# A seven-product output projection in a one-core fp32 encoder step

## The chip, the cores and the metric

The kernel runs on one core of a Trainium2 chip. The metric is the device time of one execution in microseconds. The parts of the core that matter here are TensorE (PE in the profile, with its weight loads as PEld), VectorE (DVE), ScalarE (ACT), GpSimd (POOL) and the queue on SyncE that issues the DMAs (SPq).

## The reference

One layer of a streaming encoder for 1024 prompt frames and 32 sample frames (together 1056 columns), 1024 channels. Cut to what matters here:

```
ya = (o_attn * silu(ga)) @ w_pa
yb = (silu(layernorm(conv)) * silu(gb)) @ w_pb
m  = sigmoid(ma) * ya + sigmoid(mb) * yb
y  = x + m @ w_out
```

All of it is fp32. The input projections, the attention and the depthwise convolution come ahead of these lines and are not touched.

## The kernel before

Activations lie with the channels on the 128 partitions, in eight tiles (`KT = 8`) of 1056 frames (`TT`). An fp32 operand is held as a high part and a low part, both fp32r: ScalarE writes the high part (a cast), and GpSimd or VectorE writes the remainder (a subtraction). A product of two fp32 operands is then three matmuls: high by high, low weight by high, high weight by low. One output tile of 128 channels takes 8 contraction tiles x 3 chunks of 352 frames (`CH`) x 3 matmuls = 72 matmuls, each with its own 128x128 weight load.

The end of the kernel is three such projections, each run by `outproj(g, rh, rl, mk)` over eight output tiles: `pa` (the attention branch), `pb` (the convolution branch) and `out`. In the first tile of each the contraction loop is outside the chunk loop; the other seven go through `proj`, chunk by chunk. `load_raw` (L85) brings a 512 KB weight tile by DMA into one of three rotating buffers; `split_w` casts it to `wh` on ScalarE (L91) and writes `wl` on GpSimd in three pieces (L94). The closure that `mk` returns empties PSUM:

- `mk_pa` (L1170) scales a chunk and stores it to DRAM (`s_ya`).
- `mk_pb` loads a gate tile `smb` and a `ya` tile into the pool `bg` (five buffers of 1056 frames, handed out by `big`). For each chunk VectorE does a multiply out of PSUM (L1187) and an addition (L1188) into `smb`, ScalarE writes the high part `mh` (L1189), GpSimd the low part `ml` (L1190). `mh` and `ml` are the mixed input m (doubled) of the output projection.
- `mk_out` loads the residual `xres`, adds half of the PSUM chunk to it on VectorE (L1200), and stores the chunk to `yT` (L1201).

`pb` reads its input `c_h`, `c_l` from the pool `xp`, in which the normalised input lay earlier. PSUM has eight banks, seven in `pj3` and one in `pq`; each chunk takes one.

TensorE's instructions run in the order in which they are written (`manual_schedule`). Behind the attention, the order on the other engines and on the DMA queue is set by a scheduler by priority: inside `tc.high_priority(offset=n)` an instruction counts as written n instructions earlier (2000 for weights, 4000 for emptying PSUM). A tile waits only for the readers and writers of the memory that it takes over (`reuse_waits="tile"`).

Of the kernel before, what the change touches and what calls it, by code (L numbers as in the profile page):

```python
# [8 lines left out]
F32 = mybir.dt.float32  # L9
F32R = mybir.dt.float32r  # L10
BF16 = mybir.dt.bfloat16
AF = mybir.ActivationFunctionType
ALU = mybir.AluOpType
# [5 lines left out]
TT = T + TS  # L19
# [3 lines left out]
KT = 8  # L23
CH = 352
# [5 lines left out]
LNEXP = "natural_log_exp_and_others"  # L30
NFILL = 22
R_U, R_V, R_QK, R_G, R_A = 0.25, 0.17, 0.19, 0.27, 0.12
NWARM = 46
SAT = (2, 6, 10, 14)
SKEYS = PAST + TS
# [9 lines left out]
WSP = ((0, 3), (3, 6), (6, 8))  # L45
# [3 lines left out]
def build(tc, xT, xt, wv, wf, ckT, cv, clT, stT, vec, cst, yT, kT, vO, lfO, cpT, csT):  # L49
    nc = tc.nc  # L50
# [3 lines left out]
    def pool(name, bufs=1, stack=es, **kw):  # L54
        return stack.enter_context(tc.tile_pool(name=name, bufs=bufs, reuse_waits="tile", **kw))
# [16 lines left out]
    wp = pool("wp", 2)  # L72
    lnp = pool("lnp")
    mean = lnp.tile([128, TT], F32, name="mean")
    rstd = lnp.tile([128, TT], F32, name="rstd")
    rawp = [wp]

    def f32(ap):
        return ap.bitcast(F32)

    def load_raw(key, offset=2000):
        with tc.high_priority(offset=offset):
            rawp.append(rawp.pop(0))
            raw = rawp[-1].tile([128, KT, 128], F32, name="raw", tag="raw", bufs=1)
            nc.sync.dma_start(raw, wf[WIDX[key]])  # L85
        return raw

    def split_w(raw, offset=2000):
        with tc.high_priority(offset=offset):
            wh = wp.tile([128, KT, 128], F32R, name="wh", tag="wh")  # L90
            nc.scalar.copy(wh, raw)  # L91
            wl = wp.tile([128, KT, 128], F32R, name="wl", tag="wl")
            for k0, k1 in WSP:
                nc.gpsimd.tensor_sub(wl[:, k0:k1, :], raw[:, k0:k1, :], f32(wh[:, k0:k1, :]))  # L94
        return wh, wl

    def mms(ps, w, rh, rl, sl, kts=range(KT), first=True, last=True):
        wh, wl = w
        n, N = 0, 3 * len(kts)
        for kt in kts:  # L100
            for a, b in ((wh, rh), (wl, rh), (wh, rl)):
                nc.tensor.matmul(ps, a[:, kt, :], b(kt, sl), start=(first and n == 0), stop=(last and n == N - 1))  # L102
                n += 1

    def csl(c):
        return slice(c * CH, (c + 1) * CH)
# [53 lines left out]
    def proj(*a):  # L160
        for _ in steps(*a):
            pass


    xp = pool("xp")
    xh = xp.tile([128, KT, TT], F32R, name="xh", tag="h")
    xl = xp.tile([128, KT, TT], F32R, name="xl", tag="l")
    X = lambda kt, sl: xh[:, kt, sl]
    XL = lambda kt, sl: xl[:, kt, sl]
    sg = pool("sg")  # L170

    def t352(name, bufs):
        return sg.tile([128, CH], F32, name=name, tag=name, bufs=bufs)
# [5 lines left out]
    class Banks:  # L179

        n = 0
# [5 lines left out]
    pj = Banks()  # L187
# [145 lines left out]
    order = ExitStack()  # L333
# [3 lines left out]
    with tc.high_priority(offset=9000):  # L337
# [11 lines left out]
        warm = tr.tile([128, 512], F32, name="warm", tag="tr")  # L349
        for i in range(NWARM):  # L350
            nc.tensor.matmul(warm[:, :256], idle[:, :128], idle[:, :256], start=(i == 0), stop=(i == NWARM - 1))

# [25 lines left out]
    half = slice(0, D // 2), slice(D // 2, D)  # L378
# [111 lines left out]
    V, G = nc.vector, nc.gpsimd  # L490
# [32 lines left out]
    z = zp.tile([128, 9, H], F32, name="z")  # L523
# [45 lines left out]
    for c in range(4):  # L569
# [15 lines left out]
        for t in range(8):  # L585
            ps = pj.tile([128, 512], F32, name="pjv", tag="pj")
            n = 0
            for kt in range(KT):
                sl = slice(t * 128, t * 128 + 128)
                wh, wl = wh2[kt // 4][:, kt % 4, :], wl2[kt // 4][:, kt % 4, :]  # L590
# [174 lines left out]
    def gate_steps(g, f, pj):  # L765
        def ev(c, sl, ps):
            t = t352("t", 3)
            if g == "ga":
                sides["silu"] = nc.scalar.activation(t, ps, AF.Silu)
            else:  # L770
                nc.scalar.copy(t, ps)  # L771
            nc.sync.dma_start(s_g[g][f, :, sl], t)

        return steps((g, f), X, XL, pj, ev)

    class Head:
        def __init__(self, h):
            self.h = h
# [306 lines left out]
    p3 = ExitStack()  # L1085
# [5 lines left out]
    class Banks3:  # L1091
        n = 0
# [3 lines left out]
            return (pq if self.n % 8 == 0 else pj3).tile(*a, **k)  # L1096

    pjC = Banks3()
    sg2 = pool("sg2", 4, stack=p3, side="right")
    bg = pool("bg", 5, stack=p3, side="right")  # L1100
    rawp.extend(pool(f"rw{i}", 1, stack=p3, side="right") for i in range(2))

    def big(name):
        return bg.tile([128, TT], F32, name=name, tag="big")
# [29 lines left out]
    def last_gate():  # L1134
        for _ in gate_steps(*fills.pop(0), pj3):
            pass
# [2 lines left out]
        a_half(f)  # L1139
    while fills:  # L1140
        last_gate()

    def ln_step(f):
        for g in LNO[f - 1]:
            ln_out(g)

    def outproj(g, rh, rl, mk, between=lambda f: None):

        w = split_w(load_raw((g, 0)))
        pss = [pjC.tile([128, CH], F32, name="pj", tag="pj") for _ in range(3)]  # L1150
        for kt in range(KT):
            for c in range(3):
                mms(pss[c], w, rh, rl, csl(c), range(kt, kt + 1), kt == 0, kt == KT - 1)
        ev = mk(0)
        with tc.high_priority(offset=4000):
            for c in range(3):
                ev(c, csl(c), pss[c])
        for f in range(1, 8):
            between(f)
            proj((g, f), rh, rl, pjC, mk(f))  # L1160


    def mk_pa(f):
# [8 lines left out]
        return ev  # L1172

    outproj("pa", lambda kt, sl: ah[:, kt, sl], lambda kt, sl: al[:, kt, sl], mk_pa, ln_step)
    ch_, cl_ = chl
    mh = pap.tile([128, KT, TT], F32R, name="mh", tag="h")
    ml = pap.tile([128, KT, TT], F32R, name="ml", tag="l")

    def mk_pb(f):
        smb = big("smb")  # L1180
        nc.sync.dma_start(smb, s_g["mb"][f])
        nc.scalar.activation(smb, smb, AF.Tanh, scale=0.5)
        ya = big("ya")
        nc.sync.dma_start(ya, s_ya[f])

        def ev(c, sl, ps):
            nc.vector.scalar_tensor_tensor(smb[:, sl], smb[:, sl], 1.0, ps, op0=ALU.add, op1=ALU.mult)  # L1187
            nc.vector.tensor_add(smb[:, sl], smb[:, sl], ya[:, sl])  # L1188
            nc.scalar.copy(mh[:, f, sl], smb[:, sl])  # L1189
            nc.gpsimd.tensor_sub(ml[:, f, sl], smb[:, sl], f32(mh[:, f, sl]))  # L1190
        return ev

    outproj("pb", lambda kt, sl: ch_[:, kt, sl], lambda kt, sl: cl_[:, kt, sl], mk_pb)

    def mk_out(f):
        xres = big("xres")
        nc.sync.dma_start(xres, xT[:, f, :])

        def ev(c, sl, ps):
            nc.vector.scalar_tensor_tensor(xres[:, sl], ps, 0.5, xres[:, sl], op0=ALU.mult, op1=ALU.add)  # L1200
            nc.sync.dma_start(yT[f, :, sl], xres[:, sl])  # L1201
        return ev

    outproj("out", lambda kt, sl: mh[:, kt, sl], lambda kt, sl: ml[:, kt, sl], mk_out)
    p3.close()
    es.close()

# [81 lines left out]
```

## Time and profile before

| what | us |
|---|---|
| median of 3 runs (1393.85 to 1394.35) | 1393.89 |
| span of the profiled execution, first to last instruction | 1392.1 |
| median less span: what lies around the span | 1.8 |
| PE busy in the span | 1384.3 |
| `pa`, first to last matmul that reads `ah` | 1109.7 to 1202.7 |
| `pb`, first to last matmul that reads `c_h` | 1203.1 to 1294.6 |
| `out`, first to last matmul that reads `mh` | 1295.0 to 1388.0 |

The profiled execution has no device time of its own beside its span, so its span is set against the median of the runs. A matmul's duration in the trace includes its way through the array, and consecutive matmuls overlap; what one costs in a row of them is the distance between starts.

### The profile page before, as it was taken

To read this page: it belongs to the slowest core of one execution; us is meant where nothing else is said; L and a number is where in the kernel's file an instruction comes from. 1 tells how busy PE (TensorE), PEld (TensorE's weight loads), DVE (VectorE), ACT (ScalarE), POOL (GpSimd) and SP (SyncE) were. 2 spreads that over 40 slices of the span, in tenths; PEclk is the share of its full clock that TensorE was granted. 3 is DMA by queue.
4 is the path that set the end of the run, shared out by engine and by line. 5 is a ranking of instruction groups with operands and counts; after the bars stand their busy time and mean duration, and the time that the engine had idled before them with its cause. 6 is when DMAs were issued, how large, how long until landed. Compare 5 with 4: busy or idle time off the path is not lost.

```text
span 1392.1 us, 24733 instructions
## 1 busy us (share of the span) xinstructions
PE 1384.3 (99%) x9382; PEld 1346.1 (97%) x9382; DVE 906.5 (65%) x1280; ACT 642.7 (46%) x1318; POOL 623.2 (45%) x669
## 2 busy tenths in 40 slices
PE   8999999999999999999999999999999999999999
PEld 7999999999999999999999999999999999999998
DVE  6687787888898999657766767655555487132111
ACT  6333434646464642245555556655555556222100
POOL 2324254657575875443333444343433257254320
PEclk9999999999999999999999999999999999999999
DMA  5253442424342374344545556454642779444431
GB/s 182 93 179 116 153 136 97 155 85 144 98 164 88 124 207 141 116 124 123 144 137 169 155 147 175 118 152 124 174 134 86 266 265 289 135 150 141 143 107 47
DMA packets 110615, 201.24 MB, mean 145 GB/s; under 512 B 17377, under 2 KB 74593, under 8 KB 110497
## 3 DMA queue, kind: packets, MB, share of 16 engines
q1 hardware_dynamic: 110352, 199.60, 45.7%
q8 instruction: 74, 1.21, 0.4%
q14 instruction: 45, 0.36, 0.1%
q10 hardware_dynamic: 144, 0.07, 0.0%
HBM read 129.78 MB, written 69.84 MB: 143 GB/s over the span
## 4 chain that ended last, share of the span: by engine, by line
PE 97%; DVE 1%; ACT 1%; DMA 0%; issue 0%; POOL 0%; SPq 0%; DVEq 0%; POOLq 0%; ACTq 0%
PE pj L102 71%; PE pjv L592 7%; PE ptr L966 5%; PE po L982 3%; PE po L983 3%; PE psS L938 3%; PE psS L939 2%; PE psS L941 1%; PE pst L716 1%; PE pst L715 1%; PE ptx L434 0%; DMA xtok<-xt 0%; ACT xh L436 0%; PE pjs L549 0%; DVE xl L437 0%
## 5 line engine op out<-in xcount | busy, mean ns | idle before, releaser
L102 PE MATMUL pj<-xh,wh 128*128 128x352 f32 (+2 forms) x1536 | 509.3, 332 | 0.4 <-ACT t L771 0.3
L102 PE MATMUL pj<-xl,wh 128*128 128x352 f32 (+2 forms) x1536 | 494.9, 322 | 0.2 <-DVE xl L437 0.2
L102 PE MATMUL pj<-xh,wl 128*128 128x352 f32 (+2 forms) x1536 | 493.2, 321 | 0.0
L94 POOL TENSOR_TENSOR wl<-raw,wh 128x384 fp32r<-128x384 f32 (+1 forms) x258 | 318.6, 1262 | 234.9 <-ACT wh L91 209.6
L264 DVE SCALAR_TENSOR_TENSOR y<-u,vec_t,y 128x1086 f32<-128x1086 f32 x240 | 378.3, 1577 | 11.5 <-ACT y L261 8.2
L102 PEld LDWEIGHTS pj<-xh,wh 128*128 128x128 f32 x1536 | 289.0, 188 | 3.4 <-issue 0.8
L102 PEld LDWEIGHTS pj<-xl,wh 128*128 128x128 f32 x1536 | 288.7, 188 | 1.4 <-DVE xl L437 1.2
L102 PEld LDWEIGHTS pj<-xh,wl 128*128 128x128 f32 x1536 | 289.4, 188 | 0.2 <-DVE wl L456 0.2
L949 POOL TENSOR_SCALAR P<-P,nm 128x128 f32<-128x128 f32 (+7 forms) x128 | 99.0, 773 | 230.6 <-DVE nm L948 203.1
L943 DVE TENSOR_REDUCE nm<-psS 128x1 f32<-128x128 f32 (+7 forms) x128 | 96.4, 754 | 71.9 <-PE psS L941 70.5
L91 ACT CAST wh<-raw 128x1024 fp32r<-128x1024 f32 x86 | 90.1, 1048 | 112.2 <-PE pj L102 81.0
L970 ACT CAST pth<-ptr 128x512 fp32r<-128x512 f32 (+1 forms) x192 | 89.1, 481 | 81.2 <-PE ptr L966 80.9
L971 DVE TENSOR_TENSOR ptl<-ptr,pth 128x512 fp32r<-128x512 f32 (+1 forms) x192 | 103.3, 550 | 24.0 <-ACT pth L970 22.3
L946 ACT ACTIVATE P<-psS,nm 128x128 f32<-128x128 f32 (+7 forms) x128 | 95.3, 744 | 35.0 <-DVE nm L943 30.3
L733 POOL TENSOR_TENSOR ql<-qn,qh 128x352 fp32r<-128x352 f32 (+1 forms) x48 | 64.6, 1346 | 69.2 <-ACT qh L732 49.8
L966 PE MATMUL ptr<-ident,P 128*128 128x128 f32 x576 | 85.0, 275 | 0.0
L982 PE MATMUL po<-pth,V 128*128 128x256 f32 x320 | 79.0, 283 | 0.0
L983 PE MATMUL po<-ptl,V 128*128 128x256 f32 x320 | 78.6, 281 | 0.0
L592 PE MATMUL pjv<-vwh,xh 128*128 128x260 f32 x256 | 72.5, 283 | 0.0
L592 PE MATMUL pjv<-vwl,xh 128*128 128x260 f32 x256 | 72.5, 283 | 0.0
L592 PE MATMUL pjv<-vwh,xl 128*128 128x260 f32 x256 | 72.3, 283 | 0.0
L938 PE MATMUL psS<-KB,QB 128*128 128x256 f32 (+2 forms) x192 | 67.9, 355 | 0.0
(213 smaller groups left out, 2460.8 us busy)
## 6 DMA issues: line engine op xcount, KB each, us to landing
raw<-wf SPq DMA_DIRECT2D x88, 512.0 KB
s_v<-vb SPq DMA_DIRECT2D x32, 256.0 KB
QB<-s_q SPq DMA_DIRECT2D x32, 256.0 KB
KB<-s_k SPq DMA_DIRECT2D x32, 256.0 KB
V<-s_v SPq DMA_DIRECT2D x16, 512.0 KB
kT<-qn SPq DMA_DIRECT2D x8, 528.0 KB
s_ga<-t SPq DMA_DIRECT2D x24, 176.0 KB
s_gb<-t SPq DMA_DIRECT2D x24, 176.0 KB
```

The lines of the kernel that those rows point to most:

```text
L94: nc.gpsimd.tensor_sub(wl[:, k0:k1, :], raw[:, k0:k1, :], f32(wh[:, k0:k1, :]))
L102: nc.tensor.matmul(ps, a[:, kt, :], b(kt, sl), start=(first and n == 0), stop=(last and n == N - 1))
L264: t = nc.vector.scalar_tensor_tensor(y, u[:, i:i + CW], w, y, op0=ALU.mult, op1=ALU.add)
L592: nc.tensor.matmul(ps[:, :VC], a, b, start=(n == 0), stop=(n == 23))
L938: nc.tensor.matmul(ps[:, b, :wm], QB[:, qsl], KB[:, ksl], start=True, stop=False)
L943: nc.vector.tensor_reduce(nm[:, 0:1], ps[:, :nb, :w], axis=AX.XY, op=ALU.max, negate=True)
L946: nc.scalar.activation(P[:, :nk].rearrange("p (b w) -> p b w", b=nb), ps[:, :nb, :w], AF.Exp, bias=nm[:, 0:1], accum_out=nm[:, 1:2])
L949: nc.gpsimd.tensor_scalar(P[:, :nk], P[:, :nk], nm[:, 2:3], 1.0, op0=ALU.mult, op1=ALU.mult)
L966: nc.tensor.transpose(pt[:, 128 * j:128 * j + 128], P[:, 128 * (4 * u + j):128 * (4 * u + j) + 128], ident)
L971: nc.vector.tensor_sub(ptl[:, js, qo], p3, f32(pth[:, js, qo]))
L982: nc.tensor.matmul(po[:, :256], V[:, j, :], pth[:, j, :], start=(j == 0), stop=False)
L983: nc.tensor.matmul(po[:, :256], V[:, j, :], ptl[:, j, :], start=False, stop=(j == njb - 1))
```

## The change

The output projection is done as a product of 2x2 blocks with seven products in place of eight (Strassen's, in a form with shared sums). The blocks are: the contraction in two halves of four tiles, the output channels in pairs of tiles, and the frames in two halves of 528 (`HT`, ranges `L` and `R`). Each of the seven products of a pair is 4 contraction tiles x 3 matmuls x 2 chunks of 264 frames (`HC`) = 24 matmuls. A pair has 168 matmuls of 264 columns where it had 144 of 352; in all 672 stand where 576 stood.

What is new beside the products:

- `pb` walks its tiles in the order 0, 4, 1, 5, 2, 6, 3, 7 (`PBO`), so that tiles j and j+4, which have to be combined, come one after the other.
- `form_sums(j)` makes four sums and differences of 528 frames on VectorE from mixed tiles j and j+4 (`smb`, now kept in `mixed`). One result goes to the right half of `mh`/`ml` tile j; `form_halves(j)` splits three others into `tf` tiles (three casts on ScalarE, three subtractions on VectorE). For j = 0 and 1 both are done within `pb`, for j = 2 the sums; the rest is written behind `pb`.
- The right halves of tiles 0 to 3 are no longer written by `mk_pb`.
- A pool `op` takes the memory of `xp`, after the last matmul of `pb`. It holds the second `tf` tile, two of four weight buffers, a fourth raw buffer and the partial results `u0` to `u3`.
- For each pair, `made(0)` and `made(1)` form sums of weight blocks (four VectorE operations of 512 elements) and split them, and `made(2)` splits half a tile. Each pair loads three weight tiles in place of two.
- All four pairs first do their two products on plain blocks (`first`); then each pair does its other five (`second`), with the weight sums of the next pair written between them (`then`).
- Pool order on the right side changes (`sg2` is opened last, closed after `pa`, and `tfp` takes its place), and the memory kept for dynamic DMAs is set to 1024 bytes.

```diff
+HT = TT // 2
+HC = HT // 2
+PBO = (0, 4, 1, 5, 2, 6, 3, 7)
...
+    def halves_to(h, l, t):
+        nc.scalar.copy(h, t)
+        nc.vector.tensor_sub(l, t, f32(h))
+
+    def form_sums(j):
+        a, b = mixed.pop(j), mixed.pop(j + 4)
+        t, u = (mean, rstd) if j < 3 else (big("t3"), big("u3"))
+        V = nc.vector
+        V.tensor_sub(t[:, L], a[:, R], a[:, L])
+        V.tensor_sub(u[:, L], b[:, R], a[:, R])
+        V.tensor_sub(t[:, R], b[:, R], t[:, L])
+        V.tensor_sub(u[:, R], b[:, L], t[:, R])
+        halves_to(mh[:, j, R], ml[:, j, R], u[:, L])
+        parts[j] = t[:, R], t[:, L], u[:, R]
+
+    def form_halves(j):
+        for i, t in enumerate(parts.pop(j)):
+            tf = tfs[j // 2]
+            halves_to(tf[:, i, 0, j % 2, :], tf[:, i, 1, j % 2, :], t)
...
+    outproj("pb", lambda kt, sl: ch_[:, kt, sl], lambda kt, sl: cl_[:, kt, sl], mk_pb, formed, PBO)
+    w_next = split_w(load_raw(("out", 0)))
+    pxp.close()
+    op = pool("op")
+    rawp.append(op)
+    tfs.append(op.tile([128, 3, 2, 2, HT], F32R, name="tf"))
+    homes = [op, op, wp, wp]
+    form_halves(2)
+    form_sums(3)
+    form_halves(3)
...
+    class Pair:
...
+        def made(self, i):
+            V = nc.vector
+            with tc.high_priority(offset=2000):
+                if i == 0:
+                    self.r = [load_raw(("out", 2 * self.p + n), 0) for n in range(2)]
+                    sa = self.sa = op.tile([128, KT, 128], F32, name="sa", tag="sa", bufs=1)
+                    V.tensor_add(sa[:, 4:, :], self.r[1][:, :4, :], self.r[1][:, 4:, :])
+                    V.tensor_sub(sa[:, :4, :], sa[:, 4:, :], self.r[0][:, :4, :])
+                    self.w[0] = w_tile(sa)
+                elif i == 1:
+                    sb = op.tile([128, KT, 128], F32, name="sb", tag="sb", bufs=1)
+                    V.tensor_sub(sb[:, :4, :], self.r[0][:, :4, :], self.r[1][:, :4, :])
+                    V.tensor_sub(sb[:, 4:, :], self.r[0][:, 4:, :], self.sa[:, :4, :])
+                    self.w[1] = w_tile(sb)
+                else:
+                    self.w[2] = w_tile(self.r[1][:, 4:, :], 1)
...
+        def first(self, w, x):
+            u = self.u
+            self.residual(0, 0, x)
+            self.product(w, 0, quad(0, L), lambda sl, ps: nc.scalar.copy(u[:, sl], ps))
+            nc.vector.scalar_tensor_tensor(x, u, 0.5, x, op0=ALU.mult, op1=ALU.add)
+            self.product(w, 1, quad(4, L), self.out(0, 0, x))
+
+        def second(self, then):
+            u, (sa, sb, z) = self.u, self.w
+            t1, t2 = big("r1"), big("r2")
+            x12, x21, x22, v = t1[:, L], t1[:, R], t2[:, L], t2[:, R]
+            for x, m, hf in ((x12, 0, 1), (x21, 1, 0), (x22, 1, 1)):
+                self.residual(m, hf, x)
+            half_of = lambda x, y: nc.vector.scalar_tensor_tensor(y, x, 0.5, y, op0=ALU.mult, op1=ALU.add)
+            self.product(sa, 0, form(0), lambda sl, ps: nc.vector.tensor_add(u[:, sl], u[:, sl], ps))
+            half_of(u, x21)
+            half_of(u, x12)
+            c = self.product(sa, 1, form(1), lambda sl, ps: nc.vector.tensor_add(v[:, sl], u[:, sl], ps))
+            half_of(v, x22)
+            then(0)
+            d = self.product(sb, 0, quad(0, R), self.out(1, 1, x22))
+            self.product(sb, 1, quad(4, R), self.out(0, 1, x12), c)
+            then(1)
+            self.product(self.w[2], 0, form(2), self.out(1, 0, x21), d)
+            then(2)
...
+    for p in range(4):
...
+        w = w_next
+        if p < 3:
+            with tc.high_priority(offset=2000):
+                w_next = w_tile(load_raw(("out", 2 * p + 2), 0))
+        if p > 1:
+            pairs[0].made(p - 2)
+        pairs[p].first(w, both[:, (L, R)[p % 2]])
+    pairs[0].made(2)
...
-    nc = _bacc.Bacc("TRN2", target_bir_lowering=False, num_devices=1)
+    nc = _bacc.Bacc("TRN2", target_bir_lowering=False, num_devices=1, dynamic_dma_scratch_size=1024)
```

`product` runs 4 contraction tiles for chunk 0, empties it, then chunk 1; `w_tile` is `split_w` on the four weight buffers in turn; `quad` reads `mh`/`ml`, `form` the `tf` tiles; `out` adds half of a PSUM chunk to the residual and stores 264 frames.

More of the change, by code (lines that the diff above doesn't have):

```diff
@@ L162, in proj @@
             pass
-    xp = pool("xp")
+    pxp = ExitStack()
+    xp = pool("xp", stack=pxp)
     xh = xp.tile([128, KT, TT], F32R, name="xh", tag="h")
@@ L169, in build @@
     XL = lambda kt, sl: xl[:, kt, sl]
-    sg = pool("sg")
+    psg = ExitStack()
+    sg = pool("sg", stack=psg)
     def t352(name, bufs):
@@ L1098, in build @@
     pjC = Banks3()
-    sg2 = pool("sg2", 4, stack=p3, side="right")
     bg = pool("bg", 5, stack=p3, side="right")
     rawp.extend(pool(f"rw{i}", 1, stack=p3, side="right") for i in range(2))
+    psg2 = ExitStack()
+    sg2 = pool("sg2", 4, stack=psg2, side="right")
     def big(name):
@@ L1141, in build @@
         last_gate()
+    psg.close()
     def ln_step(f):
@@ L1145, in ln_step, with outproj @@
             ln_out(g)
-    def outproj(g, rh, rl, mk, between=lambda f: None):
-        w = split_w(load_raw((g, 0)))
+    def outproj(g, rh, rl, mk, between=lambda f: None, order=range(8)):
+        w = split_w(load_raw((g, order[0])))
         pss = [pjC.tile([128, CH], F32, name="pj", tag="pj") for _ in range(3)]
@@ L1153, in outproj @@
                 mms(pss[c], w, rh, rl, csl(c), range(kt, kt + 1), kt == 0, kt == KT - 1)
-        ev = mk(0)
+        ev = mk(order[0])
         with tc.high_priority(offset=4000):
@@ L1157, in outproj @@
                 ev(c, csl(c), pss[c])
-        for f in range(1, 8):
+        for f in order[1:]:
             between(f)
@@ L1175, in build @@
     ch_, cl_ = chl
+    psg2.close()
     mh = pap.tile([128, KT, TT], F32R, name="mh", tag="h")
     ml = pap.tile([128, KT, TT], F32R, name="ml", tag="l")
+    tfp = pool("tfp", 1, stack=p3, side="right")
+    tfs = [tfp.tile([128, 3, 2, 2, HT], F32R, name="tf")]
+    L, R = slice(0, HT), slice(HT, TT)
+    mixed = {}
+    parts = {}
+    def halves_to(h, l, t):
[15 more added lines that the diff above has]
+            halves_to(tf[:, i, 0, j % 2, :], tf[:, i, 1, j % 2, :], t)
     def mk_pb(f):
-        smb = big("smb")
+        smb = mixed[f] = big("smb")
         nc.sync.dma_start(smb, s_g["mb"][f])
@@ L1188, in ev @@
             nc.vector.tensor_add(smb[:, sl], smb[:, sl], ya[:, sl])
-            nc.scalar.copy(mh[:, f, sl], smb[:, sl])
-            nc.gpsimd.tensor_sub(ml[:, f, sl], smb[:, sl], f32(mh[:, f, sl]))
-        return ev
[L1193 to L1202, printed above, removed]
@@ L1204, in build, with formed @@
-    outproj("out", lambda kt, sl: mh[:, kt, sl], lambda kt, sl: ml[:, kt, sl], mk_out)
+            sm = slice(sl.start, min(sl.stop, HT if f < 4 else TT))
+            if sm.stop > sm.start:
+                nc.scalar.copy(mh[:, f, sm], smb[:, sm])
+                nc.gpsimd.tensor_sub(ml[:, f, sm], smb[:, sm], f32(mh[:, f, sm]))
+        return ev
+    def formed(f):
+        for j in range(3):
+            if PBO.index(f) == 2 * j + 2:
+                form_sums(j)
+                if j < 2:
+                    form_halves(j)
@@ new lines, in build, with w_tile @@
+    outproj("pb", lambda kt, sl: ch_[:, kt, sl], lambda kt, sl: cl_[:, kt, sl], mk_pb, formed, PBO)
[8 more added lines that the diff above has]
+    form_halves(3)
+    def w_tile(src, n=2):
+        homes.append(homes.pop(0))
+        wh, wl = [homes[-1].tile([128, KT, 128], F32R, name=a, tag=a, bufs=2) for a in ("wh", "wl")]
+        nc.scalar.copy(wh[:, :4 * n, :], src)
+        for k0, k1 in WSP:
+            k1 = min(k1, 4 * n)
+            if k1 > k0:
+                nc.gpsimd.tensor_sub(wl[:, k0:k1, :], src[:, k0:k1, :], f32(wh[:, k0:k1, :]))
+        return wh, wl
@@ new lines, in build, with __init__, product, out @@
+    class Pair:
+        def __init__(self, p):
+            self.p = p
+            self.u = op.tile([128, HT], F32, name=f"u{p}")
+            self.w = [None] * 3
+        def made(self, i):
[14 more added lines that the diff above has]
+                    self.w[2] = w_tile(self.r[1][:, 4:, :], 1)
+        def product(self, w, half, mov, evac, pss=None):
+            wh, wl = w
+            more = pss is not None
+            pss = pss or [pjC.tile([128, CH], F32, name="pj", tag="pj") for _ in range(2)]
+            for c in range(2):
+                for kt in range(4):
+                    h, l = [m(kt, slice(c * HC, c * HC + HC)) for m in mov]
+                    k = 4 * half + kt
+                    for n, (a, x) in enumerate(((wh, h), (wl, h), (wh, l))):
+                        nc.tensor.matmul(pss[c][:, :HC], a[:, k, :], x, start=(not more and kt == 0 and n == 0),
+                                         stop=(kt == 3 and n == 2), skip_group_check=more)
+                with tc.high_priority(offset=4000):
+                    evac(slice(c * HC, c * HC + HC), pss[c][:, :HC])
+            return pss
+        def out(self, m, hf, x):
+            f = 2 * self.p + m
+            def ev(sl, ps):
+                nc.vector.scalar_tensor_tensor(x[:, sl], ps, 0.5, x[:, sl], op0=ALU.mult, op1=ALU.add)
+                nc.sync.dma_start(yT[f, :, hf * HT + sl.start:hf * HT + sl.stop], x[:, sl])
+            return ev
+        def residual(self, m, hf, x):
+            nc.sync.dma_start(x, xT[:, 2 * self.p + m, hf * HT:hf * HT + HT])
+            return x
+        def first(self, w, x):
[22 more added lines that the diff above has]
+            then(2)
@@ new lines, in quad, with form @@
+    def quad(k0, cols):
+        return [lambda kt, sl, m=m: m[:, k0 + kt, cols.start + sl.start:cols.start + sl.stop] for m in (mh, ml)]
+    def form(i):
+        return [lambda kt, sl, n=n: tfs[kt // 2][:, i, n, kt % 2, sl] for n in range(2)]
+    pairs = [Pair(p) for p in range(4)]
+    for p in range(4):
+        if p % 2 == 0:
+            both = big("r0")
+        w = w_next
[5 more added lines that the diff above has]
+        pairs[p].first(w, both[:, (L, R)[p % 2]])
@@ L1205, in build, with then @@
+    pairs[0].made(2)
+    for p in range(4):
+        def then(n):
+            if n == 0 and p < 3:
+                pairs[p + 1].made(0)
+            elif n == 1 and p < 3:
+                pairs[p + 1].made(1)
+            elif n == 2 and p < 3:
+                pairs[p + 1].made(2)
+        pairs[p].second(then)
     p3.close()
```

## The prediction

> **What bounds the kernel now.** I began with the cores (span and clock), then the page's busy times and slices, then the chain that ended last.
>
> ```profile
> core 0: 1392.1 us, clock 1.000
> PE 1384.3 (99%) x9382; PEld 1346.1 (97%) x9382; DVE 906.5 (65%) x1280; ACT 642.7 (46%) x1318; POOL 623.2 (45%) x669
> DVE  6687787888898999657766767655555487132111
> POOL 2324254657575875443333444343433257254320
> GB/s 182 93 179 116 153 136 97 155 85 144 98 164 88 124 207 141 116 124 123 144 137 169 155 147 175 118 152 124 174 134 86 266 265 289 135 150 141 143 107 47
> PE 97%; DVE 1%; ACT 1%; DMA 0%; issue 0%; POOL 0%; SPq 0%; DVEq 0%; POOLq 0%; ACTq 0%
> ```
>
> TensorE is busy for 99% of the span at the full granted clock (1.000), and it is 97% of the chain. In the last slices, those of the output projection, DVE is at 1 or 2 tenths and DMA at 47 to 143 GB/s, where 289 was reached earlier in this trace: there is room beside TensorE. The end of the chain in order of time:
>
> ```profile
> 1086.95 301.71 PE pj L102 x1872
> 1388.66 0.02 issue
> 1388.68 0.52 DVE xres L1200
> ```
>
> From 1086.95 to the end there is no gap. So time is won by issuing less matmul work, and lost only where TensorE starts to wait. What one matmul costs comes from the tile views, as last start less first start over the number of steps (three matmuls for each row's count):
>
> ```profile
> L102 PE MATMUL pj<-mh,wh x192: 318/325/331, 1295.0 to 1388.0; 128*128 128x352 f32 x192
> L102 PE MATMUL pj<-c_h,wh x192: 318/323/328, 1203.1 to 1294.6; 128*128 128x352 f32 x192
> L592 PE MATMUL pjv<-vwh,xl x68: 278/283/288, 93.7 to 117.9; 128*128 128x260 f32 x68
> L592 PEld LDWEIGHTS pjv<-vwh,xl x256: 187/188/193, 71.6 to 190.6; 128*128 128x128 f32 x128
> ```
>
> 352 columns: 93.0/(191 x 3) = 162.3 ns in the output projection, 91.5/573 = 159.7 ns in the one before it. 260 columns, with a weight load each: 24.2/(67 x 3) = 120.4 ns. The cost follows the columns, and a weight load listed at 188 ns does not stop 120 ns steps.
>
> **The products.** 576 matmuls of 162.3 ns, 93.5 us, go. 672 of 264 columns come. From 260 to 264 I add the slope between the rows, (162.3 - 120.4)/92 = 0.46 ns a column: 122.2 ns. The two 352 rows differ by 1.6% for one shape, and I don't know which kind the 260 row is, so the bounds are 120.2 and 124.3 ns: 80.8 to 83.5 us. I take 123 ns, 82.7 us. This term gives -10.8 us.
>
> **The tail.** The last PSUM chunk has 264 columns. Rows for what DVE does:
>
> ```profile
> L1200 DVE SCALAR_TENSOR_TENSOR xres<-pj,xres 128x352 f32<-128x352 f32 x23 | 12.0, 524 | 77.0 <-PE pj L102 73.6 <-POOL wl L94 3.4
> L605 DVE TENSOR_TENSOR vb<-pjv,vb x32: 404/418/426, 76.9 to 191.9; 128x256 fp32r<-128x256 f32 x32
> L1188 DVE TENSOR_TENSOR smb<-smb,ya x24: 515/526/1146, 1214.9 to 1295.8; 128x352 f32<-128x352 f32 x24
> L1115 DVE TENSOR_TENSOR al<-a,ah x8: 1246/1259/2071, 1099.9 to 1115.5; 128x1056 fp32r<-128x1056 f32 x8
> ```
>
> A PSUM chunk of 264 is near the 256 row, 0.43 us against 0.524: -0.1 us. An SBUF operation of 528 lies between 0.526 (352) and 1.246 us (1056, undisturbed): 0.71 us, and one of 512 0.69 us.
>
> **From `pb` into the output projection.** The weights for the second `first` go into memory that the last matmul of `pb` still reads, so they can't be ready before it ends.
>
> ```profile
> L91 ACT CAST wh<-raw 128x1024 fp32r<-128x1024 f32 x7 | 7.3, 1050 | 65.7 <-PE pj L102 65.7
> L94 POOL TENSOR_TENSOR wl<-raw,wh 128x384 fp32r<-128x384 f32 x14 | 14.0, 1018 | 55.5 <-ACT wh L91 55.5
> L94 POOL TENSOR_TENSOR wl<-raw,wh 128x256 fp32r<-128x256 f32 x7 | 5.2, 738 | 0.0
> L1190 POOL TENSOR_TENSOR ml<-smb,mh 128x352 fp32r<-128x352 f32 x1 | 0.9, 945 | 0.0
> ```
>
> Cast and first piece take 1.05 + 1.02 = 2.1 us; the cover is the first `first`, 48 x 0.123 = 5.9 us, whose own weights lie elsewhere. The last chunk of tile 7 is needed only by `form_sums(3)`; what that `first` reads of tile 7, 24 + 9 matmuls (4.1 us) in, came out of PSUM one chunk (24 x 0.16 = 3.8 us) before the end of `pb`. Cost nothing; without the cover 2.1 us.
>
> **What must be done before `second` starts.** The four `first` last 192 x 0.123 = 23.6 us. In them DVE has 11 operations of 528 for the forms (3 + 5 + 3), four residual additions of 528 and two of 512 for the first weight sum: 15 x 0.71 + 2 x 0.69 = 12.0 us with two SBUF inputs, and 0.5 us for tile 7. GpSimd splits four weight tiles, 4 x (2 x 1.02 + 0.74) = 11.1 us, and the last `ml`, 0.95 us. Each engine alone has room. But this trace has them in each other's way:
>
> ```profile
> 1142.23 3.50 POOL L1132 TENSOR_TENSOR c_l<-y,c_h 128x1056 fp32r<-128x1056 f32 x1
> 1143.31 3.54 DVE L1127 TENSOR_TENSOR y<-y,g 128x1056 f32<-128x1056 f32 x1
> 1146.77 1.24 DVE L1124 TENSOR_TENSOR y<-y,rstd 128x1056 f32<-128x1056 f32 x1
> ```
>
> The DVE operation that starts under GpSimd's ends 1.12 us after GpSimd does (1146.85 against 1145.73), about the 1.24 us that the next one needs with GpSimd idle: it ran nearly all of its work behind GpSimd, not beside it. If every such pair queues, 12.5 + 12.0 = 24.5 us must go one behind another in 23.6 us, 0.9 us too much. The second weight sum (1.4 + 2.8 us) and three residual additions (2.1 us) follow, due at the third product, 5.9 us later: 30.8 us in 29.5, 1.3 us too much. If nothing queues, zero. I take 1.5 us for the stall, near the queued end, because the row shows queueing.
>
> The Trainium skill, page "SBUF — State Buffer", section "Who interferes with whom", says that VectorE and GpSimd share one port pair as an exclusive lock, and that a VectorE tensor-tensor operation with both inputs in SBUF fully blocks against GpSimd's reads. The row above agrees: 3.54 against 1.24 us. By that rule alone the sum would have 1.3 us here in place of 1.5.
>
> **The pairs after that.** A `second` lasts 120 x 0.123 = 14.8 us. Beside it DVE has four weight sums and three residual additions (4.9 us) and ten PSUM chunks (4.3 us); GpSimd has two and a half splits (7.0 us). Queued port work is 11.9 us: it fits. The next pair's weights begin behind the second product, with 72 x 0.123 = 8.9 us to go. Cost nothing; 1.4 us a pair if the PSUM work queues as well (rival A).
>
> **DMA and SP.** Twelve weight loads of 512 KB, 16 residuals of 264 KB and 32 stores of 132 KB: 14.9 MB in 84 us, 177 GB/s, below the 289 above. What lies in the SP queue behind a waiting store is a later load:
>
> ```profile
> SPq L1201 <- DVE xres L1200: 69.0, 21, 6.0
> SPq L1184 <- DVE smb L1188: 43.3, 6, 9.1
> SPq L85 <- POOL wl L94: 37.6, 19, 4.0
> ```
>
> Waits there are up to 6.0 us today with TensorE unhurt; the 8.9 us cover them. Nothing; up to 2 us if several add up.
>
> **Inside `pb`.** Two `smb` tiles stay in the five buffers until their sums are made, so some loads of `ya` begin later, behind 43.3 us of such waits today. The reordered tiles cost the same matmuls. Sums and splits add at most 8 x 0.71 = 5.7 us of DVE to an 11.5 us tile (72 x 0.16) that needs 3 x (0.52 + 0.53). The cover is eight PSUM banks, each 3.8 us of matmuls. Nothing; a full bank would cost what the emptying is late, 1 to 2 us. The other pool order touches the start of `pa`, where two gate projections from 1086.95 to about 1109.7 cover the loads; nothing, a microsecond either way if that cover fails. No row shows anything that hangs on the scratch for dynamic DMAs: nothing.
>
> **Sum.** -10.8 + 1.5 - 0.1 = -9.4 us. On the span: 1392.1 to 1382.7 us. Around it lie 1.8 us (1393.89 less 1392.1), which stay: **1384.5 us**. A measurement here can tell about 0.2%, 2.8 us, from no change.
>
> **Rivals.**
>
> A, VectorE is the bound. A DVE operation blocked by GpSimd also holds the PSUM work queued behind it. Then nothing overlaps: in the four `first` 12.5 + 0.5 + 8 x 0.43 + 12.0 = 28.4 us against 23.6, 4.8 us; in three later pairs 4.9 + 4.3 + 7.0 = 16.2 against 14.8, 4.2 us. A stall of 9.0 in place of 1.5 gives 1392.0 us. For it: the rows at 1142 to 1146. Against: in slices 9 to 14 of the page DVE and POOL add up to more than ten tenths with TensorE at 9 (though a blocked operation may count as busy), and PSUM has eight banks of slack. It is that skill section's rule at its worst.
>
> B, slower: the weight sums as a chain in front of each `second`. If a weight buffer or raw buffer came free only as the pair before ends, two sums, the cast and the split (1.4 + 1.05 + 2.8 = 5.2 us) would stand open four times: +20.9 us, 1393.9 - 10.8 - 0.1 + 20.9 = 1403.9 us. It decides from a stall of 2.7 us a pair (10.8/4). For it: weight loads wait for GpSimd 19 times today. Against: four buffers rotate and a pair uses three, so the first sum of the next pair takes one that was released a product or a pair earlier.
>
> C, TensorE doesn't take the shorter matmul faster than its mean weight load, 1346.1/9382 = 143.5 ns: 672 x 0.1435 = 96.4 us, 2.9 more than now, with the stall 1398.2 us. Against: 120.4 ns at 260 columns, in a row with fresh weights each time.
>
> **How the numbers follow.** Forecast 0.73, A 0.15, B 0.09, C 0.03. A spreads from 1387 to 1392; two thirds of it lies over 2.8 us below 1393.9, a third within. Faster 0.73 + 0.10 = 0.83, same 0.05, slower 0.12. The low end has 120.2 ns and no stall: 1393.9 - 93.5 + 80.8 - 0.1 = 1381.1. The high end takes half of A in: 1389.5. Left out are B, C and the other half of A, 0.20.
>
> **What would show it.** Right: 672 matmuls of 264 columns, about 123 ns apart, some 84 us from the first on `mh` to the last, TensorE waiting 1 to 2 us in all, most of it at the first product that reads `tf` or at the third; DVE operations of 528 near 0.7 us, more under GpSimd. A would show gaps of 4 us and more at the first `second`, with DVE at 9 tenths. B would show a gap in front of each `second`, ended by `wl` or `wh`. C would show starts 143 ns apart without waits. Gaps in `pb` ended by `smb` would refute the cover there.

## The result, and the profile after

The changed kernel takes 1390.13 us in the median of six runs (1386.67 to 1391.23), the kernel before 1394.36 us. The ratio is 0.9964 with a 95% interval of 0.9953 to 0.9976: 5.0 us less by the ratio (3.3 to 6.6), where the prediction had 9.4 less. Applied to the prediction's base of 1393.89 us the ratio gives 1388.9 us.

The cores and the busy times of after:

```profile
core 0: 1388.2 us, clock 0.999
PE 1374.9 (99%) x9478; PEld 1336.3 (96%) x9478; DVE 975.4 (70%) x1368; ACT 660.0 (48%) x1346; POOL 653.3 (47%) x685
DVE  6687788878898999647666766655555488156773
```

The span is 3.9 us shorter (1392.1 to 1388.2). VectorE's last three slices, those of the output projection, were at 1 tenth each before and are now at 7, 7 and 3. The tile views of after place the time:

```profile
L105 PE MATMUL pj<-ah,wh x192: 318/325/425, 1110.5 to 1206.8; 128*128 128x352 f32 x192
L105 PE MATMUL pj<-c_h,wh x192: 318/322/327, 1207.3 to 1298.7; 128*128 128x352 f32 x192
L1290 PE MATMUL pj<-mh,wh x128: 281/284/389, 1299.2 to 1381.6; 128*128 128x264 f32 x128
L1290 PE MATMUL pj<-tf,wh x192: 278/284/289, 1323.5 to 1384.7; 128*128 128x264 f32 x192
```

From the first matmul on `mh` to the VectorE operation behind the last matmul there are 85.9 us (1299.2 to 1385.05, below) where there were 93.7 (1295.0 to 1388.68): -7.8 us. The convolution projection is as long as it was (91.4 us, before 91.5). But the attention projection, whose code is untouched, takes 96.3 us where it took 93.0: +3.3 us. It also begins 0.8 us later; over the traces of this study that start lies between 1109.5 and 1110.5, so I don't count it as the change's. -7.8 + 3.3 + 0.8 gives -3.7; the convolution projection (-0.1) and the stretch from the last VectorE operation to the end (3.2 us, before 3.4) bring it to the 3.9 us of the span, within rounding.

What TensorE waited for, by the waits view of after (line, releaser, us in total, times, longest); none of these four lines is there before:

```profile
PE pj L1290 <- DVE r L1325: 2.6, 1, 2.6
PE pj L105 <- ACT wh L94: 2.1, 1, 2.1
PE pj L1290 <- DVE r L1300: 0.7, 1, 0.7
PE pj L105 <- POOL wl L97: 0.7, 1, 0.7
```

So TensorE stands idle for 3.3 us in the output projection and 2.8 us in the attention projection. (Counted from start to start a wait costs a little more, as the matmul behind it can't overlap with the one before: the 2.1 and 0.7 us cost the 3.3 us by which the attention projection grew.) L1300 empties a PSUM chunk into the output, L1325 is `v = u + c` in `second`.

**The attention projection.** The DMA queue in order of time, before and then after. In both, `raw` is a weight load, `smb` and `ya` are loads for the convolution projection.

```profile
1172.75 0.32 SPq L1181 DMA_DIRECT2D smb<-s_mb  x1
1173.87 0.32 SPq L1184 DMA_DIRECT2D ya<-s_ya  x1
1177.54 0.32 SPq L1181 DMA_DIRECT2D smb<-s_mb  x1
...
1180.35 0.37 SPq L85 DMA_DIRECT2D raw<-wf  x1
```

```profile
1173.56 0.32 SPq L1214 DMA_DIRECT2D smb<-s_mb  x1
...
1181.41 0.42 SPq L1217 DMA_DIRECT2D ya<-s_ya  x1
1181.92 0.38 SPq L1214 DMA_DIRECT2D smb<-s_mb  x1
1182.41 0.37 SPq L88 DMA_DIRECT2D raw<-wf  x1
1182.83 0.99 SPq L1178 DMA_DIRECT2D s_ya<-sma  x2
1190.72 0.80 SPq L1173 DMA_DIRECT2D sma<-s_ma  x2
```

The second `ya` load, which stood right behind its `smb` at 1173.87, comes at 1181.41. With the new tile order the second tile needed is tile 4, which the attention projection, still in the order 0 to 7, stores only in its fifth turn. Now `ya`, `smb` and `raw` (528, 528 and 512 KB) are issued within 1.4 us, two small stores behind them, and the queue stands from 1183.8 to 1190.7 until a store has landed that frees an `sma` buffer. ScalarE's and TensorE's timelines of after show the end of it:

```profile
1193.02 0.50 ACT L1174 ACTIVATE sma<-sma 128x352 f32<-128x352 f32 x1 [2.94 <-DMA sma<-s_ma]
1193.43 1.03 ACT L94 CAST wh<-raw 128x1024 fp32r<-128x1024 f32 x1
1194.51 0.42 PE L105 MATMUL pj<-ah,wh 128*128 128x352 f32 x1 [2.10 <-ACT wh L94]
```

The weight cast stands on ScalarE behind an operation that waits for the late `sma` load, and TensorE for the cast.

**The output projection.** VectorE's first operations in it:

```profile
1300.48 0.71 DVE L1201 TENSOR_TENSOR u<-smb 128x528 f32<-128x528 f32 x1
1301.10 1.53 DVE L1202 TENSOR_TENSOR t<-smb,t 128x528 f32<-128x528 f32 x1
1302.67 1.41 DVE L1203 TENSOR_TENSOR u<-smb,t 128x528 f32<-128x528 f32 x1
1304.01 2.68 DVE L1194 TENSOR_TENSOR tf<-mean,tf 128x528 fp32r<-128x528 f32 x2
...
1317.04 0.76 DVE L1300 SCALAR_TENSOR_TENSOR r<-pj,r 128x264 f32<-128x264 f32 x2
```

and GpSimd's operation beside them:

```profile
1300.49 12.27 POOL L1253 TENSOR_TENSOR wl<-raw,wh 128x384 fp32r<-128x384 f32 x9 [2.32 <-ACT wh L1249]
```

One operation of 528 takes 0.71 us, and 1.2 to 1.5 us while GpSimd splits weights. The first PSUM chunks that VectorE has to empty are emptied at 1317.04, by which time, counting the chunks, all eight banks are full: that is the 0.7 us wait. Two of the eight hold chunks for ScalarE, which emptied its first four by 1308.5 and then stood before a cast of `sa`, the weight sum that VectorE had not finished (how much of the 0.7 us this makes was not tested):

```profile
1316.61 1.04 ACT L1249 CAST wh<-sa 128x1024 fp32r<-128x1024 f32 x1 [8.14 <-DVE sa L1271]
```

The 2.6 us wait is read from the chain that ended last:

```profile
1320.22 4.75 POOL wl L1253 x4
...
1326.40 0.96 DVE sb L1276
...
1327.81 5.92 DMA raw<-wf
...
1333.85 0.09 DVE sa L1270
...
1334.52 0.43 DVE r L1325
...
1335.00 50.03 PE pj L1290 x408
...
1385.05 0.43 DVE r L1300
```

GpSimd's splits hold up `sb` of pair 1; only then are its buffers free, and a weight tile of pair 2 is loaded into one (5.92 us). The first weight sum of pair 2, `sa`, waits for that load, and it stands on VectorE **ahead** of L1325 of pair 0, without which TensorE can't start the fourth product. From 1335.00 on there is no gap.

### The profile page after: what moved, and what is told of

Its sections match the earlier page's. It is cut to its first block, busy times and chain, and to the rows that moved or that the text cites. A ratio compares the mean times of both kernels' runs of the same rounds, so it can differ in the third digit from the quotient of the medians.

```text
span 1388.2 us, 25134 instructions
## 1 busy us (share of the span) xinstructions
PE 1374.9 (99%) x9478; PEld 1336.3 (96%) x9478; DVE 975.4 (70%) x1368; ACT 660.0 (48%) x1346; POOL 653.3 (47%) x685
## 5 line engine op out<-in xcount | busy, mean ns | idle before, releaser
L97 POOL TENSOR_TENSOR wl<-raw,wh 128x384 fp32r<-128x384 f32 (+1 forms) x237 | 307.5, 1325 | 185.7 <-ACT wh L94 163.2
L94 ACT CAST wh<-raw 128x1024 fp32r<-128x1024 f32 x79 | 82.8, 1048 | 50.7 <-PE pj L105 21.6
L993 DVE TENSOR_TENSOR ot<-ot,po 64x256 f32<-64x256 f32 x64 | 26.7, 417 | 59.7 <-ACT ot L992 59.0
```

## The experiments

**1. The tile order alone, and 2. the pools alone**, both on the kernel before. The edit of the first is shown, with `PBO` for the order 0, 4, 1, 5, 2, 6, 3, 7.

```diff
-    outproj("pb", ..., mk_pb)
+    outproj("pb", ..., mk_pb, order=PBO)
```

> The kernel before, with one edit: the convolution projection walks its tiles in the order 0, 4, 1, 5, 2, 6, 3, 7; the output projection stays plain. Theory O (the order costs the attention projection its last weights: the ya tile 4 that is now needed second is stored late, so its load, a gate load and a weight load stand together in the DMA queue): a wait of TensorE of 2 to 3 us near the end of the attention projection, ended by wh or wl; first to last matmul on ah about 96 us instead of 93.0; time about 1397 us against 1394.4. Rival P (the pools' new order and the smaller DMA scratch are the cause): no wait there, 93 us, 1394.4 us.

> The kernel before, with the pools of after only: sg2 opened last on the right side and closed after the attention projection, pools xp and sg on stacks of their own, 1024 bytes for dynamic DMAs; tiles and products as before. Theory O: no new wait, first to last matmul on ah 93 us, 1394.4 us. Rival P: a wait of 2 to 3 us near the end of the attention projection, 1397 us.

The order alone takes 1396.60 us, ratio 1.0019 (1.0010 to 1.0027); the pools alone 1394.65 us, ratio 1.0001 (0.9993 to 1.0010). The waits view of the first:

```profile
PE pj L103 <- ACT wh L92: 1.2, 1, 1.2
PE pj L103 <- POOL wl L95: 0.7, 1, 0.7
```

The same two waits, 1.9 us in this execution, with a plain output projection behind them; the second has neither. The order makes this loss, the pools don't.

**3. The attention projection in the same order**, on the changed kernel, so that each `ya` tile is stored in the order in which it is needed.

```diff
-    outproj("pa", ..., mk_pa, ln_step)
+    outproj("pa", ..., mk_pa, lambda f: ln_step(PBO.index(f)), PBO)
```

> The changed kernel, with the attention projection walking its tiles in the same order 0, 4, 1, 5, 2, 6, 3, 7 as the convolution projection, so that each ya tile is stored in the order in which it is needed. Theory O: the waits of 2.1 and 0.7 us in the attention projection go, 93 us from first to last matmul on ah, time 1390.1 - 2.8 = 1387.3 us, and a smaller spread than the 4.6 us of the changed kernel. Rival P: they stay, 96 us, 1390 us.

1387.85 us, ratio 0.9944 (0.9930 to 0.9957): 2.3 us below the changed kernel. In the DMA queue `smb` and `ya` are neighbours again, and the waits in the attention projection are gone; the two of the output projection stay:

```profile
1172.65 0.43 SPq L1214 DMA_DIRECT2D smb<-s_mb  x1
1173.75 0.32 SPq L1217 DMA_DIRECT2D ya<-s_ya  x1
```

```profile
PE pj L1290 <- DVE r L1325: 3.0, 1, 3.0
PE pj L1290 <- DVE r L1300: 0.7, 1, 0.7
```

The intervals of this one and of the changed kernel overlap, so the 2.3 us rest on the trace as well: the attention projection takes 93.4 us (1109.5 to 1202.9) against 96.3. The spread, 2.4 us over five runs against 4.6 over six, is smaller, as expected.

The trace also holds a loss that the waits view doesn't list. Behind the 3.0 us wait, from about 1332.2 to 1335.6, TensorE is granted half its clock, and matmuls of 264 columns start 0.22 us apart where they otherwise take 0.122. A row of the windows view, and two starts:

```profile
core 0: us, PE busy (x) PEld busy (x) DVE busy (x) ACT busy (x) POOL busy (x), PEclk, DMA share, GB/s
1333.00:1334.00 1.00, 1.00 (x6) 1.00 (x6) 0.90 (x4) 0.00 (x0) 0.00 (x0) 0.50 0.99 365
```

```profile
1333.14 0.42 PE L1290 MATMUL pj<-mh,wh 128*128 128x264 f32 x1
1333.36 0.42 PE L1290 MATMUL pj<-mh,wl 128*128 128x264 f32 x1
```

Some 15 matmuls at 0.22 us are about 1.5 us. So in this execution the output projection is longer than in the changed kernel (87.5 us from first to last start, against 85.5), and the spans differ by only 1.9 us. Behind the 2.6 us wait of the changed kernel the clock stays at 1.00. What sets the drop off isn't shown: one execution has it. Three of the five runs, the profiled one among them, took 1387.85 to 1388.10 us and two took 1385.67 and 1385.77; whether the drop makes this difference isn't shown either.

**4. VectorE in written order** from the first `second` on.

```diff
     pairs[0].made(2)
+    es.enter_context(tc.manual_schedule(engines={E.PE, E.DVE}))
```

> The changed kernel, with VectorE held to the written order from the first second() on, so that the weight sums of pairs 1 to 3 stand behind the PSUM work of the pair before and are not pulled ahead. Theory Q (VectorE's queue: a weight sum that waits for its weight DMA stands ahead of the PSUM work that TensorE needs): the waits of TensorE of 2.6 us (at the fourth product of pair 0) and 0.7 us (at the fourth first()) both go, first to last matmul of the output projection about 82.8 us instead of 85.9, time 1390.1 - 3.3 = 1386.8 us. Rival L (the port shared by VectorE and GpSimd alone: the same work takes as long in any order): the two waits stay or move, 85 to 86 us, 1390 us.

1385.80 us, ratio 0.9937 (0.9925 to 0.9950), clear of the changed kernel's interval. VectorE in pair 0 of this kernel:

```profile
1327.87 0.43 DVE L1325 TENSOR_TENSOR r<-u,pj 128x264 f32<-128x264 f32 x1 [0.79 <-PE pj L1290]
1328.34 0.71 DVE L1321 SCALAR_TENSOR_TENSOR r<-r 128x528 f32<-128x528 f32 x1
1328.96 0.69 DVE L1270 TENSOR_TENSOR sa<-raw 128x512 f32<-128x512 f32 x1
```

The weight sum now stands behind L1325, and the 2.6 us wait is gone; from first to last start the output projection takes 82.7 us (1297.5 to 1380.2) against 85.5. The 0.7 us wait stays, against what I expected: it comes from the four `first`, which this edit doesn't order. The time fell by 4.3 us where 3.3 were expected; the waits in the attention projection, 1.2 us in this execution, are no fixed amount.

**5. No low parts of weights on GpSimd**, on the changed kernel. What is left out stands in the expectation.

```diff
-                nc.gpsimd.tensor_sub(wl[:, k0:k1, :], src[:, k0:k1, :], f32(wh[:, k0:k1, :]))
+                nc.gpsimd.memset(f32(wl[:, k0:k1, :]), 0.0)
```

> The changed kernel without part of its computation: the low parts of the output projection's weights (from the second weight tile on) are filled with zeros by GpSimd instead of subtracted, so GpSimd no longer reads SBUF there; everything else as it was. Theory L1 (VectorE's operations with two SBUF inputs queue behind GpSimd's reads): between the end of the convolution projection and the first product on tf the VectorE operations of 528 frames take 0.70 us each instead of 1.2 to 1.5, the first emptying of a first() comes several us earlier than 14 us behind its matmuls, and the wait of 0.7 us at the fourth first() goes. Rival (these operations are slow on VectorE by themselves, or wait for ScalarE's casts): they stay at 1.2 to 1.5 us and the wait stays. The wait of 2.6 us hangs on a weight DMA in front of the PSUM work: by theory Q it may move, but is not explained by the port. Time 1387 to 1390 us.

1384.49 us, ratio 0.9931 (0.9918 to 0.9945). VectorE and GpSimd in this kernel:

```profile
1298.93 0.70 DVE L1202 TENSOR_TENSOR t<-smb,t 128x528 f32<-128x528 f32 x1
1304.13 1.46 DVE L1194 TENSOR_TENSOR tf<-mean,tf 128x528 fp32r<-128x528 f32 x1
```

```profile
1297.11 2.98 POOL L1253 MEMSET wl<- 128x384 f32 x9 [1.13 <-PE pj L105]
1303.97 1.06 POOL L1225 TENSOR_TENSOR ml<-smb,mh 128x352 fp32r<-128x352 f32 x1
```

L1202 took 1.53 us in the changed kernel, beside GpSimd's subtraction. Here it takes 0.70 us, although it lies wholly beside GpSimd's `memset`, which writes the same tiles but reads none. The operation at 1304.13 starts under the one subtraction that GpSimd still does there, and takes 1.46 us. So what slows VectorE here is what GpSimd reads.

Both waits of the output projection are gone, the 2.6 us one too: weights and buffers come early enough that the order on VectorE does no harm. The edit can't tell two causes of that apart: GpSimd no longer reads, and its own pieces of 384 became shorter (0.42 us in the mean, where those on `raw` took 1.30). The time lies below my 1387 to 1390 us, since I had not expected that. Of the 5.6 us below the changed kernel, about 1.5 are waits in the attention projection, 1.3 us in this execution against 2.8.

**6. Both repairs (3 and 4), and 7. the forms spread as well.** In 7, VectorE is in written order from the end of the convolution projection, and the forms stand between the four `first`:

```diff
+    es.enter_context(tc.manual_schedule(engines={E.PE, E.DVE}))
     form_halves(2)
-    form_sums(3)
-    form_halves(3)
...
-        if p > 1:
-            pairs[0].made(p - 2)
+        if p == 2:
+            pairs[0].made(0)
+            form_halves(3)
         pairs[p].first(w, both[:, (L, R)[p % 2]])
+        if p == 0:
+            form_sums(3)
+    pairs[0].made(1)
     pairs[0].made(2)
```

> The changed kernel with both repairs: the attention projection's tiles in the order 0, 4, 1, 5, 2, 6, 3, 7, and VectorE in written order from the first second() on. If the two losses are separate, their repairs add: 2.8 and 2.6 us against the changed kernel, no wait in the attention projection, one of 0.7 us in the output projection, time about 1384.5 us; first to last matmul on ah 93.0 us. If they were one loss seen twice (all of it DMA landing late), the second repair adds nothing to the first: 1386 to 1388 us.

> As the one with both repairs, and VectorE in written order from the end of the convolution projection on, with the forms spread between the four first(): the halves of tile 2, the emptying of the first first(), the sums of tile 3, the emptying of the second, the first weight sum, the halves of tile 3, then the other two. Theory: the 0.7 us wait comes from PSUM being emptied 14 us late; with the emptying in between it goes, and nothing else moves: no wait of TensorE in the output projection, time 1383.8 us, 0.7 us below the one before it. Rival: the serial port work (24.5 us by the rows of before, in 23.6 us) only moves the wait to the first second(), where tf or wh then comes late: a wait of 1 us or more there, 1384.5 us or more.

With both repairs 1383.35 us (1383.05 to 1383.93), ratio 0.9923 (0.9910 to 0.9937): the repairs add, and only the 0.7 us wait is left. With the forms spread 1382.40 us, ratio 0.9917 (0.9903 to 0.9930): the fastest version, 11.6 us below the kernel before by the ratio. The step from 6 to 7 is inside the intervals; the trace shows it, as no wait of TensorE is left from the attention projection on:

```profile
L1289 PE MATMUL pj<-mh,wh x128: 281/284/288, 1295.2 to 1373.7; 128*128 128x264 f32 x128
L1289 PE MATMUL pj<-tf,wh x192: 278/284/289, 1318.4 to 1376.8; 128*128 128x264 f32 x192
```

672 matmuls in 81.6 us from first to last start: 121.6 ns each. The rival for 7, a wait that only moves to the first `second`, did not come.

## Why the prediction was right, and where it was not

**The number.** By the ratio the time is 1388.9 us, 4.4 us above the forecast of 1384.5 and inside the range of 1381.1 to 1389.5, near its high end. That it is inside is in part luck. The high end came from half of rival A, a stall on VectorE alone; but of the 6.1 us of waits 2.8 lie in a projection where the sum had nothing, and 2.6 hang on a weight load that it also had at nothing.

**The products: right.** The rows gave 122.2 ns and I took 123; it is 121.6. Against the old 162.3 ns this is 93.5 to 81.7 us, -11.8 us where the prediction had -10.8. Rival C (143 ns) is refuted.

**The stall in the output projection: right in kind, wrong in make-up.** I had 1.5 us for the queueing of VectorE and GpSimd; the waits are 3.3 us. The queueing itself is shown by 5 (1.53 us against 0.70 for the same operation). The Trainium skill, page "SBUF — State Buffer", section "Who interferes with whom", adds that a two-input VectorE operation contends only with GpSimd's reads. The trace of 5 agrees: 0.70 us beside GpSimd's writes, 1.46 us beside its reads. But the queueing alone makes only the 0.7 us: with the same queueing and VectorE in written order (4) nothing else is left. The 2.6 us need the order on VectorE as well. The sum left out who stands behind a held-up operation. My 24.5 us of port work against 23.6 looked only at what is due before `second`; in the trace the forms and pair 0's weight sums stood ahead of the first emptying of PSUM, and ScalarE behind them (0.7 us), and a sum of pair 2 was pulled ahead into pair 0's `second` (2.6 us). The first is rival A's mechanism, at 0.7 us where A had 9.0; the second has a weight DMA in it.

**DMA and SP: the step failed.** I costed it at nothing because 8.9 us cover a late load. The cover held for the weights: no wait in the output projection was ended by `wh` or `wl`, so rival B didn't occur. It did not hold for VectorE's queue, in which another pair's weight sum, waiting for its load, stood ahead of PSUM work that was due. I had asked what a late load delays for its own pair, and not what is queued behind the instruction that waits for it.

**Inside `pb`: the step failed.** "The reordered tiles cost the same matmuls", with eight PSUM banks as cover, was true of the convolution projection. The cost appeared one projection earlier: the order changes which `ya` has to be stored when, and the load that depends on it moved in the DMA queue to where the last weights of the attention projection are fetched. It is 1.9 us by the trace of 1 (2.6 by its ratio) and 2.8 us by the trace of the changed kernel. The forms themselves cost nothing there.

**From `pb` into the output projection, and the tail: right.** No wait at the boundary. The tail, from the start of the last VectorE operation to the end of the span, is 3.2 us (1385.05 to 1388.2) against 3.4.

What stays open: whether the weight cast at 1193.43 waited only for the `sma` operation ahead of it or for its own load too, which the records don't tell apart; and how large the waits are in executions without a profile, where times went from 1386.67 to 1391.23 us.

## What to carry to other kernels

When tiles are reordered, follow each tile back to the stage that writes it: a load through DRAM can only be issued once its store is done, and where it lands in the queue it delays others. When work is added to an engine that has time to spare, price what is queued behind each of its waits; here the written order took 2.8 us off the output projection with the same instructions. And an operation's price must be read from rows in which its neighbour engine does what it will do in the new place.

## What the runs showed of the hardware

A VectorE operation of 528 with two SBUF inputs took 0.70 us beside a GpSimd operation that only writes (5), and 1.2 to 1.5 us beside one that reads (the changed kernel).

Behind a TensorE wait of 3.0 us the granted clock was 0.50 for about 3.4 us (3); behind one of 2.6 us it stayed at 1.00 (the changed kernel). One execution each.

The spread of the run times did not tell these losses here. The changed kernel's six runs differ by 4.6 us, the eleven of 1 by 5.7, and the five with both repairs by 0.9. But the 21 runs of the kernel before that stand beside 1 to 4 differ by 2.9 us, and its trace has none of these waits; the five runs of 4, which keeps the waits in the attention projection, differ by 1.3.
